# One decoder step on one core: three input projections in the loop that makes the token operands instead of two, with the raw tokens packed three pieces to a tile

## The chip, the core and the metric

The kernel runs on one core of one Trainium2 chip. A core has five engines with an instruction queue each: PE (TensorE, matmuls and weight loads), DVE (VectorE), ACT (ScalarE), POOL (GpSimd) and SP (SyncE, here only an issuer of DMAs); ACT and POOL issue DMAs too. The metric is the device time of one execution in microseconds (us); lower is better. Before, it is 1874.0 us, the median of three runs.

## What is computed

The reference is one inference step of a hybrid decoder layer for 1024 prompt tokens and 8 sample tokens, 1032 in all, of 1024 numbers each, in fp32. Cut to what this case touches:

```
def project_inputs(x, l, w):
    z = rmsnorm(x, w['attn_norm_g'][l]) @ w['w_in'][l]          # rmsnorm(x) = x * rsqrt(mean(x*x) + 1e-6) * gain
    q, kc, vc, ks, vs, kw, vw, nsa_g, pool_u, mem_q, merge_g = jnp.split(z, _split_points(), axis=-1)
    q = rmsnorm(q.reshape(b, t, KV_HEADS, GROUP, HEAD_DIM), w['nsa_q_g'][l])     # per head of 64
    ks = rmsnorm(kv(ks), w['nsa_ks_g'][l])
    kw = rmsnorm(kv(kw), w['nsa_kw_g'][l])
```

Behind it come three attention branches, a pooling mixer, a merge, an output projection and a feed-forward network; the change touches none of them.

## The kernel before

**Layout.** Tokens lie along the free axis, 1032 wide, in three chunks of 344 (`CH`); the 1024 features lie on 128 partitions in `KD` = 8 pieces (k = 0 to 7). Each fp32 operand is split into a high part and a low remainder in fp32r (a format of TensorE's), and each product is three matmuls: high weights by high tokens, high by low, low by high. One projection of 128 outputs over one chunk is thus 8 x 3 = 24 matmuls into one PSUM tile.

**The front.** The loop over chunks (L330 to L359) loads the raw tokens `xr` piece by piece (even k by SP, odd k by ACT), and makes of each piece: its high part `xh` on ACT (L338), its low part `xl` on DVE (L339), its square on POOL for odd k and on ACT for even k (L345, L347), and the running sum `ssq` of the squares on DVE for odd k and on POOL for even k (L348). The same loop runs two projections, ks and kw (weights `w_p[0]`, `w_p[1]`), over these operands: 2 x 24 matmuls for each chunk (L354). After a chunk, a matmul of `ssq` with ones (`ps_p`, L356) sums over the partitions, and `rsqrt` makes 1/rms of it in `rstd`: L273 on DVE, three ACT instructions (L274 to L276), L277 and L278 on DVE. Two multiplications by `rstd` bring the products into `z` (L359).

**Behind the front.** `hnorm` (from L368) normalises ks and kw per head; then four query projections q0 to q3 follow in `proj` (its matmuls are in `gemm`, L257; its low weights are L240, its multiplication by `rstd` L364), each with its `hnorm`. One unit of `hnorm` is one chunk of one projection: a square and a cast on ACT, a subtraction on POOL, two matmuls (L380), then `rsqrt` again and a final multiplication on DVE (L383). Six projections by three chunks make 18 units. Then come nine token blocks of the value projection (matmuls L257 with `wvh`, `wvl`), whose PSUM tiles DVE empties into `vtok` (L437) and `gate` (L438).

**Memory and order.** SBUF tiles of 1032 columns come from a ring of `NT` = 12 buffers, PSUM tiles from rings with tags g, s, t and p of 1, 3, 3 and 1 (`PSB`). Instructions are written in program order, and the framework's scheduler reorders them on each engine by a simulated timeline, so that an edit at one place moves rows elsewhere too.

Of the kernel before, what the change touches and what calls it, by code (L numbers as in the profile page):

```python
# [9 lines left out]
AF = mybir.ActivationFunctionType  # L10
ALU = mybir.AluOpType
# [5 lines left out]
KD = D // 128  # L17
# [4 lines left out]
CW = max(n for _, n in CH)  # L22
# [171 lines left out]
def body(nc, tc, xT, memT, w_p, w_m, w_v, w_mk, w_mv, w_up, w_un, w_out, w_gu, w_dn, w_pool, w_cmp, gains, consts, jlt,  # L194
         pg_k, pg_v, win_k, win_v, cm_k, cm_v, st_p, pt, ptv, o_y, o_k, o_v, o_wk, o_wv, o_pu, o_ps, o_mk, o_mv):
    from contextlib import ExitStack, nullcontext
    V, S, G, PE, SY = nc.vector, nc.scalar, nc.gpsimd, nc.tensor, nc.sync
    f = lambda a: a.bitcast(F32)
# [13 lines left out]
    def XG(name):  # L212
        return xgp.tile([128, T], F32R, name=name, tag="xg", bufs=16)
# [13 lines left out]
    ones = cp.tile([128, 128], F32, name="ones")  # L227
# [4 lines left out]
    def gv(n, i=0):  # L232
        return gn[:, _GW[n][0] + i:_GW[n][0] + i + 1]

    def psum(tag="s", dt=F32, w=512):
        return pp.tile([128, w], dt, name="ps_" + tag, tag=tag, bufs=dict(zip(('g', 's', 't', 'p'), PSB))[tag])

    def split(src, hi, lo, he=None, le=None):
        (he or S.copy)(hi, src)  # L239
        (le or V.tensor_sub)(lo, src, f(hi))  # L240

    def wload(src, n, eng=None, le=None, parts=1):
        wr = wp.tile([128, n], F32, name="wr", tag="wr", padded_shape=[128, T])
        (eng or SY).dma_start(wr, src)
        wh = wp.tile([128, n], F32R, name="wh", tag="wh", padded_shape=[128, 1024])
        wl = wp.tile([128, n], F32R, name="wl", tag="wl", padded_shape=[128, 1024])
        for i in range(parts):
            c = slice(n // parts * i, n // parts * (i + 1))
            split(wr[:, c], wh[:, c], wl[:, c], le=le)
        return wh, wl  # L250
# [31 lines left out]
    ca = A.enter_context(tc.tile_pool(name="cstA", bufs=1))  # L282
    CWID = consts.shape[1]
    ct = ca.tile([128, CWID], F32, name="ct")
    G.dma_start(ct, consts)

    def C(n):
        o, w, r = _CW[n]
# [7 lines left out]
    def TT(dt=F32, name="t"):  # L296
        return st_["tp"].tile([128, T], dt, name=name, tag="T", bufs=NT)
# [12 lines left out]
    def TX(name):  # L310
        return st_["tp"].tile([128, 512], F32R, name=name, tag="X", bufs=NX)
# [2 lines left out]
                                               engine=mybir.EngineType.Activation, ins=[], outs=[]))  # L314


    xh, xl, xr = [], [], []
    ssq = TT(name="ssq")
    rstd = cp.tile([128, T], F32, name="rstd")
    W01 = []  # L320
    ks, kw = TT(name="z"), TT(name="z")

    def xload(k, c):
        (SY, S)[k % 2].dma_start(xr[k][:, c], xT[k][:, c])

    for k in range(KD):
        xr.append(TT(name="xr"))
        xh.append(XG("xh"))
        xl.append(XG("xl"))
    for ci, (c0, n) in enumerate(CH):  # L330
        c = slice(c0, c0 + n)
        pss = [psum("st"[ci % 2])[:, :n] for _ in range(2)]
        for k in range(KD):
            xload(k, c)
            if ci == 0 and k < 2:
                W01.append(wload(w_p[k], 1024, parts=2))
            h, l = xh[k][:, c], xl[k][:, c]
            S.activation(h, xr[k][:, c], AF.Copy, scale=gv("attn", k))  # L338
            V.scalar_tensor_tensor(l, xr[k][:, c], gv("attn", k), f(h), op0=ALU.mult, op1=ALU.subtract)  # L339
            if k == 0:  # L340
                S.activation(ssq[:, c], xr[k][:, c], AF.Square)
            else:
                sq = TU("sq")[:, :n]
                if k in XG_SQ:
                    G.tensor_mul(sq, xr[k][:, c], xr[k][:, c])  # L345
                else:
                    S.activation(sq, xr[k][:, c], AF.Square)  # L347
                (G if k in XG_ADD else V).tensor_add(ssq[:, c], ssq[:, c], sq)  # L348
        for k in range(KD):
            for t in range(2):  # L350
                wh, wl = W01[t]
                w = slice(k * 128, k * 128 + 128)
                for x, (a, b) in enumerate(((wh, xh), (wh, xl), (wl, xh))):
                    PE.matmul(pss[t], lhsT=a[:, w], rhs=b[k][:, c], start=k == 0 and x == 0, stop=k == KD - 1 and x == 2)  # L354
        ps = psum("p")[:, :n]
        PE.matmul(ps, lhsT=ones, rhs=ssq[:, c], start=True, stop=True)  # L356
        rsqrt(tmp, rstd[:, c], ps, n, 1.0 / D)
        for t, z in enumerate((ks, kw)):
            V.tensor_mul(z[:, c], pss[t], rstd[:, c])  # L359

    def proj(i, src=None, tag="t"):
        wh, wl = wload((w_p if src is None else src)[i], 1024)
        z = TT(name="z")
        gemm(wh, wl, xh, xl, KD, lambda ci, c0, n, ps: V.tensor_mul(z[:, c0:c0 + n], ps, rstd[:, c0:c0 + n]),  # L364
             tag)
        return z
# [24 lines left out]
    ps = psum("g")  # L391
# [16 lines left out]
    qall = ca.tile([128, 64], F32, name="qall")  # L408
    V.memset(qall, 0.0)
    for j in range(4):  # L410
        q = proj(2 + j)
        hnorm(q, blk64, 1 / 64, gv("q"), split_sq=True)
        for s in range(2):
            h = 2 * j + s
            V.tensor_copy(qall[(h // 4) * 64:(h // 4) * 64 + 64, h * 8:h * 8 + 8], q[s * 64:s * 64 + 64, TP:T])
        SY.dma_start(qd[j], q)
# [5 lines left out]
    for a, b in ((0, 3), (3, 6), (6, 8)):  # L422
        n = (b - a) * 280
        r = TT(name="wvr")
        SY.dma_start(r[:, :n], w_v[:, a * 280:b * 280])
        h, l = TT(F32R, "wvh"), TT(F32R, "wvl")
# [4 lines left out]
    for t in range(9):  # L431
        m = 128 if t < 8 else NB
        c = slice(t * 128, t * 128 + m)
# [1067 lines left out]
```

## Time and profile before

| | before |
|---|---|
| median of three runs | 1874.0 us (1872.23 to 1876.44) |
| profiled execution | 1869.54 us |
| its span, first to last instruction | 1867.8 us |
| mean granted TensorE clock | 0.989 of full speed |
| PE busy | 1798.3 us, 96% of the span |
| DVE, ACT, POOL busy | 1210.0, 870.7, 737.5 us |
| first matmul | 7.67 us after the start |
| last matmul of the front (L354) | 48.27 us after the start |
| PE's next idle time behind it | before 116.08 us, 1.33 us long |

The profile is one execution seen by the hardware profiler; its time is 0.24% under the median of the three runs. PE is busy for nearly the whole span, so a change of the time has to come out of the idle time and the slow stretches that are left to PE. A row of the time line names its start in us, its length, the engine, the line of the code, and the operation as output<-inputs.

### The profile page before, as it was taken

Reading aid. Unit: us, or ns where it says so; the run is one execution under the profiler, and the core shown is the slowest. Engines: PE = TensorE matmul, PEld = TensorE weight load, DVE = VectorE, ACT = ScalarE, POOL = GpSimd, SP = SyncE. Lnnn points to the kernel's source line nnn. Section 1 sums busy time; section 2 is a strip of 40 time slices with the busy share of each in tenths; the row PEclk is TensorE's granted clock in tenths of the full one; section 3 lists DMA queues with packets and bytes.
Section 4 is the critical chain, followed back from the end, with each engine's and each line's share of the span. In section 5 each row is a group of like instructions: output and inputs, shape, how many; then the busy total and the mean of one; then the engine's idle time right before and its main releaser. Section 6 shows DMA issues by size and latency. Waiting matters only on the chain.

```text
span 1867.8 us, 34509 instructions
## 1 busy us (share of the span) xinstructions
PE 1798.3 (96%) x12337; PEld 1729.2 (93%) x12337; DVE 1210.0 (65%) x2748; ACT 870.7 (47%) x2012; POOL 737.5 (39%) x865
## 2 busy tenths in 40 slices
PE   6999999999999999989999999999999999999999
PEld 5998998888988999979989998899999999999999
DVE  8875788663564766778886834866666666636332
ACT  5643766445454676657774545422322223314100
POOL 5300211556341645457753437655545545100000
PEclk9999999899999999989999999999999999999999
DMA  4243124999665111552325643122222222546122
GB/s 162 100 148 139 65 101 164 296 316 315 205 201 169 53 43 63 179 165 78 108 64 177 213 134 100 62 87 78 71 80 80 84 87 69 170 131 184 59 69 94
DMA packets 142366, 241.13 MB, mean 129 GB/s; under 512 B 21449, under 2 KB 100450, under 8 KB 142194
## 3 DMA queue, kind: packets, MB, share of 16 engines
q1 hardware_dynamic: 118722, 189.69, 31.2%
q0 software_dynamic: 8496, 30.23, 4.8%
q10 hardware_dynamic: 14976, 19.01, 2.9%
q8 instruction: 97, 1.59, 0.4%
q14 instruction: 75, 0.61, 0.1%
HBM read 176.31 MB, written 62.55 MB: 128 GB/s over the span
## 4 chain that ended last, share of the span: by engine, by line
PE 55%; DMA 5%; DVE 4%; issue 2%; ACT 2%; POOL 1%; SPq 0%; ACTq 0%; DVEq 0%; POOLq 0%
PE ps_t L257 10%; PE ps_s L1385 10%; PE ps_t L1385 9%; PE ps_g L257 7%; PE ps_s L257 7%; PE ps_p L1061 3%; PE ps_s L1032 3%; PE ps_t L1077 2%; PE ps_g L1385 2%; PE ps_p L1385 2%; DMA mg<-acd 1%; DMA mg<-gd 1%; DMA gt<-gd 1%; DMA olr<-od 1%; DVE t L240 0%
## 5 line engine op out<-in xcount | busy, mean ns | idle before, releaser
L257 PE MATMUL ps_g<-xh,wh 128*128 128x344 f32 x624 | 206.1, 330 | 3.9 <-ACT mg L543 2.3
L257 PE MATMUL ps_g<-xl,wh 128*128 128x344 f32 x624 | 201.7, 323 | 0.0
L257 PE MATMUL ps_g<-xh,wl 128*128 128x344 f32 x624 | 201.6, 323 | 0.0
L239 ACT CAST wh<-wr 128x512 fp32r<-128x512 f32 (+3 forms) x138 | 99.9, 746 | 199.9 <-PE ps_t L257 83.5
L1051 POOL TENSOR_SCALAR P<-P,st,gate 128x384 f32<-128x384 f32 (+2 forms) x192 | 125.6, 664 | 94.6 <-DVE st L1046 37.8
L240 DVE TENSOR_TENSOR wl<-wr,wh 128x512 fp32r<-128x512 f32 (+3 forms) x112 | 105.0, 946 | 56.9 <-ACT wh L239 55.5
L239 ACT CAST cw<-tS 128x512 fp32r<-128x512 f32 x88 | 54.3, 619 | 182.0 <-PE ps_t L1385 98.2
L522 ACT ACTIVATE P<-P,st 128x384 f32<-128x384 f32 (+2 forms) x192 | 112.1, 586 | 40.1 <-DVE st L519 36.3
L257 PEld LDWEIGHTS ps_g<-xh,wh 128*128 128x128 f32 x624 | 118.2, 189 | 9.2 <-ACT mg L543 4.1
L257 PEld LDWEIGHTS ps_g<-xl,wh 128*128 128x128 f32 x624 | 118.5, 190 | 1.1 <-issue 0.4
L257 PEld LDWEIGHTS ps_g<-xh,wl 128*128 128x128 f32 x624 | 118.2, 189 | 1.3 <-issue 0.2
L240 DVE TENSOR_TENSOR ptl<-ps_t,pth 128x512 fp32r<-128x512 f32 (+1 forms) x208 | 108.0, 530 | 15.6 <-ACT pth L239 13.4
L239 ACT CAST pth<-ps_t 128x512 fp32r<-128x512 f32 (+1 forms) x208 | 91.3, 457 | 46.6 <-PE ps_t L1077 29.2
L240 DVE TENSOR_TENSOR cw<-tS,cw 128x512 fp32r<-128x512 f32 x88 | 93.3, 1061 | 29.7 <-ACT cw L239 26.1
L1385 PE MATMUL ps_s<-t,cw 128*128 128x258 f32 x792 | 106.1, 283 | 3.1 <-ACT rq L274 3.1
L1385 PE MATMUL ps_t<-t,cw 128*128 128x258 f32 x792 | 106.8, 283 | 2.1 <-DVE t L240 2.1
L1385 PE MATMUL ps_s<-b,cw 128*128 128x258 f32 x792 | 107.8, 286 | 0.0
L1385 PE MATMUL ps_t<-b,cw 128*128 128x258 f32 x792 | 105.6, 282 | 0.3 <-issue 0.3
L1385 PEld LDWEIGHTS ps_s<-t,cw 128*128 128x128 f32 x792 | 100.0, 190 | 3.3 <-ACT rq L274 3.3
L1385 PEld LDWEIGHTS ps_t<-t,cw 128*128 128x128 f32 x792 | 99.6, 189 | 2.9 <-DVE t L240 2.9
L1385 PEld LDWEIGHTS ps_s<-b,cw 128*128 128x128 f32 x792 | 101.4, 192 | 0.3
L519 DVE CUSTOM_DVE_ANT_0 P<-ps_s,ct 128x384 f32<-128x384 f32 (+3 forms) x160 | 83.2, 530 | 27.0 <-PE ps_t L1077 18.1
(527 smaller groups left out, 5659.0 us busy)
## 6 DMA issues: line engine op xcount, KB each, us to landing
kpg<-pg_k SPq DMA_DIRECT2D x128, 192.0 KB, 4.1
wr<-w_gu SPq DMA_DIRECT2D x44, 512.0 KB, 3.8
gd<-mg ACTq DMA_DIRECT2D x72, 172.0 KB, 3.4
wr<-w_m POOLq DMA_DIRECT2D x24, 512.0 KB, 5.4
acd<-zu SPq DMA_DIRECT2D x44, 258.0 KB, 2.0
mg<-acd SPq DMA_DIRECT2D x66, 172.0 KB, 3.0
mg<-gd SPq DMA_DIRECT2D x48, 172.0 KB, 2.4
wr<-w_p SPq DMA_DIRECT2D x16, 512.0 KB, 3.4
```

The lines of the kernel that those rows point to most:

```text
L239: (he or S.copy)(hi, src)
L240: (le or V.tensor_sub)(lo, src, f(hi))
L257: PE.matmul(ps, lhsT=x, rhs=y, start=i == 0, stop=i == n - 1)
L519: V.tensor_tensor_reduce(P[u], s, m, -scale, ini, ALU.add, ALU.min, st[:, u:u + 1])
L522: S.activation(P[u], P[u], AF.Exp, bias=nm, scale=-1.0, accum_out=st[:, 6 + u:7 + u])
L1032: PE.matmul(ps, lhsT=u["q"][:, i * 128:i * 128 + 128], rhs=kk[:, k0 * 128 + a:k0 * 128 + a + n], start=x == 0, stop=x == 1)
L1051: lastp[:] = [G.tensor_scalar(p_, p_, st4[:, j, 5:6], gate[:, q, c:c + 1], op0=ALU.mult, op1=ALU.mult)]
L1061: PE.matmul(pv[:, c0:c0 + n], lhsT=lh, rhs=rhs, start=pvs["n"] == 0, stop=last, skip_group_check=True)
L1077: PE.transpose(pt_[:, x * 128:x * 128 + 128], pd[y][:, o - offs[y]:o - offs[y] + 128], ident)
L1385: PE.matmul(ps[c], lhsT=a[:, x * 512 + k * 128:x * 512 + k * 128 + 128], rhs=b[k][:, y * HT + c * HC:y * HT + c * HC + HC], start=first an ...
```

## The change

Four edits, all in the front:

1. The raw tokens of one chunk are packed three pieces to one tile of 1032 columns, so three tiles a chunk in place of eight tiles for all chunks. The third chunk's second and third tile take the buffers of the first chunk's first two.
2. A third projection, q0 (weights `w_p[2]`), joins ks and kw in the loop. Its weights are loaded to a tile of their own (`wraw`) and split in two halves of 512 columns (`halves`). Its 24 matmuls of a chunk are written behind the 48 of the other two, and `ps_p` stands among them. The later `proj(2)` falls away.
3. The PSUM tiles of the chunks come from tags s, t, s; the three of a chunk take all three buffers of their tag.
4. The load of the constants `ct` is written behind the first chunk's operands, no longer ahead of the front. On POOL's queue it still stands second, right behind the load of the gains.

Matmuls, vector operations and bytes moved are the same in number, but for the split of q0's weights (two halves on each of ACT and DVE in place of one whole instruction).

```
-    G.dma_start(ct, consts)
...
     for ci, (c0, n) in enumerate(CH):
         c = slice(c0, c0 + n)
-        pss = [psum("st"[ci % 2])[:, :n] for _ in range(2)]
+        xt = [TT(name="xr") for _ in range(3)]
+        if ci == 0:
+            ssq = TT(name="ssq")
+            zs = [TT(name="z") for _ in range(3)]
+        pss = [psum("sts"[ci])[:, :n] for _ in range(2)]
         for k in range(KD):
-            xload(k, c)
+            xr = xt[k // 3][:, k % 3 * CW:k % 3 * CW + n]
+            (SY, S)[k % 2].dma_start(xr, xT[k][:, c])
...
+        if ci == 0:
+            SY.dma_start(raw[:, :1024], w_p[2])
+            W.append(halves(raw, lambda: TX("w2")))
+            G.dma_start(ct, consts)
+
+        def along(t, k):
+            wh, wl = W[t]
+            for x, (a, b) in enumerate(((wh, xh), (wh, xl), (wl, xh))):
+                PE.matmul(pss[t], lhsT=a(k), rhs=b[k][:, c], start=k == 0 and x == 0, stop=k == KD - 1 and x == 2)
+
         for k in range(KD):
             for t in range(2):
...
+                along(t, k)
+        pss.append(psum("sts"[ci])[:, :n])
+        for k in range(KD):
+            along(2, k)
+            if k == 3:
+                ps = psum("p")[:, :n]
+                PE.matmul(ps, lhsT=ones, rhs=ssq[:, c], start=True, stop=True)
         rsqrt(tmp, rstd[:, c], ps, n, 1.0 / D)
-        for t, z in enumerate((ks, kw)):
+        for t, z in enumerate(zs):
             V.tensor_mul(z[:, c], pss[t], rstd[:, c])
+    ks, kw, q0 = zs
...
-        q = proj(2 + j)
+        q = proj(2 + j) if j else q0
```

The lines move: the front's matmuls from L354 to L367, `xh` L338 to L348, `xl` L339 to L349, `ssq` L348 to L358, `ps_p` L356 to L377, its `z` L359 to L380, the token loads L324 to L343, `hnorm`'s L380 and L383 to L402 and L405, `vtok` and `gate` L437 and L438 to L459 and L460. What the scheduler makes of it is seen at three places.

**ACT, around the second chunk's token loads.** Before, ACT issues the loads of all three chunks (L324) between the casts of the first; `xr_161`, `xr_167`, `xr_173` and `xr_179` are the pieces k = 1, 3, 5 and 7, and the last rows shown are the last loads:

```order
L338 ACTIVATE xh_162<-xr_161,gn_139 128x344
L347 ACTIVATE sq_213<-xr_164 128x344
L324 DMA xr_161<-xT 128x344
L338 ACTIVATE xh_165<-xr_164,gn_139 128x344
L347 ACTIVATE sq_225<-xr_170 128x344
L324 DMA xr_167<-xT 128x344
L338 ACTIVATE xh_168<-xr_167,gn_139 128x344
L347 ACTIVATE sq_237<-xr_176 128x344
L324 DMA xr_173<-xT 128x344
L338 ACTIVATE xh_171<-xr_170,gn_139 128x344
L338 ACTIVATE xh_165<-xr_164,gn_139 128x344
L324 DMA xr_179<-xT 128x344
```

Of the changed kernel, these are the rows at the end of the first chunk; `ps_p_313` is that chunk's sum of squares, `xr_338` and `xr_339` are tiles of the second chunk:

```order
L348 ACTIVATE xh_167<-xr_173,gn_139 128x344
L239 CAST w2_243<-wraw_154 128x512
L348 ACTIVATE xh_169<-xr_173,gn_139 128x344
L239 CAST w2_247<-wraw_154 128x512
L274 ACTIVATE rq_a_328<-ps_p_313,epst_143 128x344
L275 ACTIVATE rstd_153<-rq_a_328 128x344
L276 ACTIVATE rq_a_328<-rstd_153 128x344
L343 DMA xr_338<-xT 128x344
L343 DMA xr_339<-xT 128x344
L348 ACTIVATE xh_155<-xr_338,gn_139 128x344
L351 ACTIVATE ssq_174<-xr_338 128x344
L343 DMA xr_339<-xT 128x344
```

The second chunk's loads on ACT now stand behind the three `rsqrt` instructions of the first.

**DVE, at the border of the first and the second chunk.** Before, around the first chunk's `rsqrt` (`rq_w_296`, and `rstd_155` with its two `z`), low parts and sums of the later chunks stand between its steps:

```order
L348 TENSOR_TENSOR ssq_154<-ssq_154,sq_339 128x344
L348 TENSOR_TENSOR ssq_154<-ssq_154,sq_435 128x344
L339 SCALAR_TENSOR_TENSOR xl_181<-xr_179,gn_139,xh_180 128x344
L712 TENSOR_SCALAR ptr_3815<-ptr_3815,ct_148 128x16
L277 TENSOR_TENSOR rq_w_296<-rq_w_296,rq_a_297 128x344
L348 TENSOR_TENSOR ssq_154<-ssq_154,sq_351 128x344
L278 SCALAR_TENSOR_TENSOR rstd_155<-rq_w_296,rstd_155 128x344
L348 TENSOR_TENSOR ssq_154<-ssq_154,sq_447 128x344
L359 TENSOR_TENSOR z_156<-ps_s_182,rstd_155 128x344
L359 TENSOR_TENSOR z_157<-ps_s_183,rstd_155 128x344
```

Of the changed kernel, `rq_w_327` is the first chunk's; `xr_338` is the second chunk's first tile:

```order
L358 TENSOR_TENSOR ssq_174<-ssq_174,sq_239 128x344
L273 TENSOR_SCALAR rq_w_327<-ps_p_313 128x344
L277 TENSOR_TENSOR rq_w_327<-rq_w_327,rq_a_328 128x344
L278 SCALAR_TENSOR_TENSOR rstd_153<-rq_w_327,rstd_153 128x344
L380 TENSOR_TENSOR z_175<-ps_s_178,rstd_153 128x344
L380 TENSOR_TENSOR z_176<-ps_s_179,rstd_153 128x344
L380 TENSOR_TENSOR z_177<-ps_s_300,rstd_153 128x344
L349 SCALAR_TENSOR_TENSOR xl_156<-xr_338,gn_139,xh_155 128x344
L358 TENSOR_TENSOR ssq_174<-ssq_174,sq_350 128x344
L349 SCALAR_TENSOR_TENSOR xl_158<-xr_338,gn_139,xh_157 128x344
```

All of `rsqrt` and three multiplications of the first chunk now stand ahead of the first low part of the second.

**PE, around the second chunk's `ps_p`.** Before, `ps_s_414` and `ps_s_415` are ks and kw of the third chunk; 24 matmuls of `ps_s_415` follow behind these rows, and then q0's projection:

```order
L354 MATMUL ps_s_414<-xh_180,wh_187 128x344
L354 MATMUL ps_s_414<-xl_181,wh_187 128x344
L354 MATMUL ps_s_414<-xh_180,wl_188 128x344
L356 MATMUL ps_p_402<-ssq_154,ones_141 128x344
L394 MATMUL ps_g_527<-ct_148,rstd_155 128x1 x2
L354 MATMUL ps_s_415<-xh_159,wh_199 128x344
L354 MATMUL ps_s_415<-xl_160,wh_199 128x344
L354 MATMUL ps_s_415<-xh_159,wl_200 128x344
```

Of the changed kernel, `ps_t_437` is the third projection of the second chunk, and `ps_s_478` the first of the third:

```order
L367 MATMUL ps_t_437<-xh_167,w2_248 128x344
L367 MATMUL ps_t_437<-xh_169,w2_247 128x344
L367 MATMUL ps_t_437<-xl_170,w2_247 128x344
L377 MATMUL ps_p_450<-ssq_174,ones_141 128x344
L367 MATMUL ps_t_437<-xh_169,w2_248 128x344
L367 MATMUL ps_s_478<-xh_155,wh_183 128x344
L367 MATMUL ps_s_478<-xl_156,wh_183 128x344
L367 MATMUL ps_s_478<-xh_155,wl_184 128x344
```

All 72 matmuls of the third chunk now stand behind the second chunk's `ps_p`, whose input is the sum `ssq` of that chunk. On DVE that sum's last addition (`ssq_174<-ssq_174,sq_386`) stands behind all but one of the third chunk's low parts, in these rows:

```order
L349 SCALAR_TENSOR_TENSOR xl_162<-xr_476,gn_139,xh_161 128x344
L349 SCALAR_TENSOR_TENSOR xl_164<-xr_476,gn_139,xh_163 128x344
L349 SCALAR_TENSOR_TENSOR xl_166<-xr_476,gn_139,xh_165 128x344
L349 SCALAR_TENSOR_TENSOR xl_168<-xr_477,gn_139,xh_167 128x344
L358 TENSOR_TENSOR ssq_174<-ssq_174,sq_386 128x344
L349 SCALAR_TENSOR_TENSOR xl_170<-xr_477,gn_139,xh_169 128x344
L358 TENSOR_TENSOR ssq_174<-ssq_174,sq_499 128x344
```

Behind the front, the first matmuls of `hnorm` (L402) stand 30 matmuls of the next projection behind the last of the front; before, the first one stands one matmul behind it (`ps_t_669` is then q0, now it is q1 in `ps_t_819` and `ps_t_845`).

## Rows read from the trace of the kernel before

**Rows 1.** The page's list of busy time by engine (us, share, instructions).

```profile
PE 1798.3 (96%) x12337; PEld 1729.2 (93%) x12337; DVE 1210.0 (65%) x2748; ACT 870.7 (47%) x2012; POOL 737.5 (39%) x865
```

**Rows 2.** PE's waits from 0 to 130 us: in total, times, longest.

```profile
PE ps_s L354 <- ACT xh L338: 7.7, 1, 7.7
PE ps_s L354 <- ACT wh L239: 3.0, 1, 3.0
PE ps_p L356 <- DVE ssq L348: 2.1, 1, 2.1
PE ps_t L354 <- DVE xl L339: 1.9, 3, 0.8
PE ps_t L257 <- DVE gate L438: 1.3, 1, 1.3
```

**Rows 3.** Windows: start:end and length, busy us (instructions) by engine, granted clock, DMA.

```profile
core 0: us, PE busy (x) PEld busy (x) DVE busy (x) ACT busy (x) POOL busy (x), PEclk, DMA share, GB/s
...
8.00:48.40 40.40, 31.61 (x152) 27.91 (x152) 36.53 (x55) 21.78 (x45) 24.46 (x22) 0.96 0.43 150
...
42.00:45.90 3.90, 3.90 (x14) 3.57 (x15) 3.90 (x7) 2.40 (x5) 2.50 (x2) 0.56 0.01 2
...
51.23:115.30 64.07, 63.52 (x413) 62.67 (x412) 54.84 (x103) 47.25 (x98) 17.58 (x17) 1.00 0.36 134
...
62.00:115.30 53.30, 52.75 (x341) 51.95 (x339) 47.75 (x87) 39.65 (x80) 15.09 (x14) 1.00 0.40 151
...
70.00:110.00 40.00, 40.00 (x267) 40.00 (x266) 38.41 (x70) 29.03 (x60) 11.28 (x10) 1.00 0.46 169
...
116.00:400.00 284.00, 270.29 (x1664) 253.76 (x1664) 201.32 (x510) 150.18 (x372) 66.31 (x124) 0.98 0.48 165
```

**Rows 4.** PE's time line at the front's end and the gate: start, length, idle before.

```profile
41.96 1.04 PE L356 MATMUL ps_p<-ssq,ones 128*128 128x344 f32 x2 [2.09 <-DVE ssq L348]
...
48.11 0.32 PE L354 MATMUL ps_s<-xl,wh 128*128 128x344 f32 x1
48.27 0.33 PE L354 MATMUL ps_s<-xh,wl 128*128 128x344 f32 x1
48.44 0.32 PE L257 MATMUL ps_t<-xh,wh 128*128 128x344 f32 x1
...
116.08 0.37 PE L257 MATMUL ps_t<-wvh,xh 128*128 128x280 f32 x1 [1.33 <-DVE gate L438]
```

**Rows 5.** Groups of instructions, 0 to 48 us: busy us, mean ns.

```profile
L339 DVE SCALAR_TENSOR_TENSOR xl<-xr,gn,xh 128x344 fp32r<-128x344 f32 x24 | 20.3, 880 | 0.7 <-ACT xh L338 0.4 <-DMA xr<-xT 0.3
L348 DVE TENSOR_TENSOR ssq<-ssq,sq 128x344 f32<-128x344 f32 x12 | 9.3, 777 | 0.8 <-POOL ssq L348 0.8
L240 DVE TENSOR_TENSOR wl<-wr,wh 128x512 fp32r<-128x512 f32 x4 | 3.2, 830 | 2.1 <-ACT wh L239 2.1
L274 ACT ACTIVATE rq_a<-ps_p,epst 128x344 f32<-128x344 f32 x2 | 1.1, 545 | 4.2 <-DVE rq_w L273 4.2
```

**Rows 6.** DVE's time line in the front, and its first `hnorm` and gate instructions.

```profile
8.65 0.57 DVE L339 SCALAR_TENSOR_TENSOR xl<-xr,gn,xh 128x344 fp32r<-128x344 f32 x1
...
13.09 1.07 DVE L339 SCALAR_TENSOR_TENSOR xl<-xr,gn,xh 128x344 fp32r<-128x344 f32 x1
...
17.78 4.22 DVE L339 SCALAR_TENSOR_TENSOR xl<-xr,gn,xh 128x344 fp32r<-128x344 f32 x4
...
43.44 0.50 DVE L273 TENSOR_SCALAR rq_w<-ps_p 128x344 f32<-128x344 f32 x1
...
51.23 0.51 DVE L273 TENSOR_SCALAR rq_w<-ps_s 128x344 f32<-128x344 f32 x1
...
115.30 0.48 DVE L437 TENSOR_SCALAR vtok<-ps_t,rtok 128x256 f32<-128x256 f32 x1
```

**Rows 7.** ACT's last token load of the front on its queue.

```profile
18.35 0.33 ACTq L324 DMA_DIRECT2D xr<-xT  x1
```

**Rows 8.** Token loads of the first 48 us by queue: count, KB, us to landing.

```profile
xr<-xT SPq DMA_DIRECT2D x12, 172.0 KB, 2.3
xr<-xT ACTq DMA_DIRECT2D x12, 172.0 KB, 3.8
```

**Rows 9.** DVE's groups from 48.4 to 116 us.

```profile
L364 DVE TENSOR_TENSOR z<-ps_t,rstd 128x344 f32<-128x344 f32 x12 | 6.1, 510 | 0.9 <-PE ps_t L257 0.8
L240 DVE TENSOR_TENSOR wl<-wr,wh 128x1024 fp32r<-128x1024 f32 x5 | 6.1, 1220 | 1.6 <-ACT wh L239 1.6
L359 DVE TENSOR_TENSOR z<-ps_s,rstd 128x344 f32<-128x344 f32 x2 | 0.9, 512 | 0.0
```

## What the change should do to the time

> **What bounds the kernel now.** The page's busy times come first [rows 1]: PE works for 96% of the span, so about 69 us of it are PE's own idle time, and the change can only win out of that, or out of stretches where PE runs slowly. PE's waits of the first 130 us [rows 2] show where it idles here. Before its first matmul it waits 7.7 us for the first `xh` and then 3.0 us for weights; after that the list is only DVE's: 3.5 us in all for low parts `xl`, and 2.1 us at the second chunk's `ps_p` for `ssq`. So the front's pace is set by DVE. The windows say the same [rows 3]: from 8 to 48.4 us DVE is busy for 36.5 of 40.4 us, PE for 31.6. And those 31.6 are not all at full speed: after the wait of 2.09 us at `ps_p` [rows 4] the granted clock is 0.56 of full speed between 42 and 45.9 us [rows 3], near the lower of its two levels, 1.2 of 2.4 GHz.
>
> From 48.44 us on, where the front's last matmul is out [rows 4], PE has work without a gap until it waits 1.33 us for DVE's `gate` at 116.08. Between, DVE is not idle either: 54.84 us of the 64.07 from the first `hnorm` step to the first evacuation of the value blocks, and 38.41 of 40 us (96%) from 70 to 110 [rows 3]. So two chains of nearly one length meet at 116 us: PE's matmuls, and DVE's `hnorm` steps. The change has to shorten both to win.
>
> **Step 1: what leaves PE behind the front.** q0's 72 matmuls move into the front. A matmul of this shape starts 0.16 us behind the one ahead (48.11, 48.27, 48.44) [rows 4]: 72 x 0.157 = 11.3 us. The third chunk's `ps_p`, which lies behind the front before and inside it now, is about 0.5 us more (half of the pair that takes 1.04 us in [rows 4]). So if the front now ends less than 11.8 us later than 48.4, that is before 60.2 us, PE gets to the gate earlier, else later. The change pays on PE only as far as the added matmuls fill idle time.
>
> **Step 2: when the front now ends.** I walk along DVE, which sets its pace. The first chunk: 8 low parts at 0.88 us, 4 sums at 0.78, and 6 halves of weights at 0.83 (two of them new, for q0) are 15.1 us [rows 5]; from about 8 us on [rows 6], with no wait for tokens, that is 23 us. Now comes the border of the chunks. In the order of before DVE goes on with later chunks there. In the new order it stands still: `ps_p` (0.5 us, in PE's queue behind nearly all of the third projection's 24 matmuls) and then `rsqrt` with three ACT instructions of 0.55 us or a little less [rows 5], 1.5 us together, leave it idle for about 3 us; its own L273, L277, L278 and three `z` of 0.5 us are 3 us more. That makes 29 us. On ACT the second chunk's odd loads stand behind the same `rsqrt`, so they go out at about 27 us where before the last of all three chunks was out at 18.35 [rows 7]; with 2.3 to 3.8 us to landing [rows 8] they are there at 29.5 to 31, which costs another 0.5 us. So the second chunk's first low part starts at 29.5 us.
>
> From there to the last sum of the second chunk DVE's order has 15 low parts and 5 sums: 13.2 + 3.9 = 17.1 us, so `ps_p` starts at 46.6 us; before it started at 41.96 [rows 4]. PE has nine matmuls for each piece now, 1.4 us, where DVE needs 1.1 to 1.3 for a piece's low part and its share of the sums: the second chunk's 72 go along from 30 us on and are out at 42 to 44 us, so PE waits, I estimate, 3 us for `ssq`, longer than the 2.09 us of before. Behind `ps_p` lie all 72 matmuls of the third chunk, the last of the second, and the third chunk's `ps_p`. At full clock that is 73 x 0.157 + 2 x 0.5 = 12.5 us and 0.6 us for the small products L416; and the slow stretch comes again: 14 matmuls in 3.9 us [rows 3] in place of 2.2, 1.7 us more. 46.6 + 12.5 + 0.6 + 1.7 = **61.4 us**, 1.2 us behind the 60.2 of step 1.
>
> The bounds: a low part takes 0.57 us where POOL rests and 1.07 where POOL works [rows 6]. 15 of them at 0.57 give 56.8 us for the front's end, at 1.07 64.3 us. The four in a row of 4.22 us [rows 6] stand near the upper price.
>
> **The rule that bears on that price.** The Trainium skill says on its page "SBUF — State Buffer", section "SBUF: two separate sides", that a VectorE instruction with two SBUF inputs and a GpSimd instruction that reads SBUF take one port pair in turn, whichever starts first holding it throughout. The two durations above agree with that. By the rule alone the front would end at the upper bound, since POOL's squares of the second chunk now start together with that chunk's low parts, and the time would be 1879.5 us.
>
> **Step 3: DVE's chain to the gate.** The first `hnorm` matmuls of the new order stand 30 matmuls behind the front's end, 4.7 us; before one matmul. So DVE's first `hnorm` step comes at about 61.4 + 5 = 66.4 us, where it came at 51.23 [rows 6]. From there it has less left than before: the 54.84 us of [rows 3] lose four multiplications of `proj` (2.0), the third chunk's two `z` (0.9), one whole weight remainder (1.2) [rows 9], and L277, L278 of the third chunk's `rsqrt` and the two `rtok` copies (1.4 by 0.5 us each): 5.5 us, 49.3 left. All 18 units of `hnorm` bar one still stand ahead of the first gate evacuation on DVE. At the 96% of the stretch 70 to 110 that takes 51.4 us: the evacuation starts at 66.4 + 51.4 = **117.8 us**, against 115.30 [rows 6], 2.5 us later. At the 90% of 62 to 115.3 (47.75 of 53.30) [rows 3] it takes 54.8 us, 5.9 us later. I take the higher share, as all units' squares are then long made and only DVE is short, and lean a little to the other: 3 us.
>
> PE arrives by step 2 at 114.75 + 1.2, about 116 us, so it waits there for DVE: the gate, not PE, decides, and the delay is 3 us. What follows is PE's: 270.3 of 284 us busy from 116 to 400 [rows 3], with waits on what is behind it in the same order, so the delay is carried to the end. Edits without a price: the packing moves the same 24 loads of 172 KB [rows 8]; the constants' load keeps its place on POOL's queue; the PSUM tags give each chunk three buffers, which the third chunk takes from the first, long multiplied by then.
>
> **The sum.** 1869.54 + 3 = 1872.5 us for an execution like the profiled one. That one lies 4.5 us under the median of the three runs, so against the median the forecast is 1874.0 + 3 = **1877 us**. 0.2% of it, 3.7 us, is about what a measurement of this kernel can tell from no change; the forecast is thus no change, leaning to slower.
>
> **Rivals.** *The front hides the third projection (faster).* The low parts of the later chunks come at their lower price, or the border costs less than I think: DVE's own work of the front, 8 + 36.5 us and 1.7 for the two halves, would let it end near 49 to 50 us. Then PE saves up to 11 us, and DVE's chain starts at 55, gate at 106: -10 us, 1864 us. It decides from a front that ends at 55.5 us: 60.5 + 51.4 = 111.9, 3.4 us won. Against it stand the order's rows at the border and at the second `ps_p`. Chance 0.22, with -4 to -6 us likelier than -10.
>
> *The gate comes later still (slower).* Low parts at the upper price put the front's end at 64.3 us and the gate at 69.3 + 51.4 = 120.7, 5.4 us later; DVE's share at 90% makes it 5.9, both 8.8. And PE, idle at the gate for 3 us and more, restarts at the lower clock, another 1.7 us by the same 14 matmuls. That is 1879.5 to 1884.5 us. It decides from a gate evacuation behind 119.0 us. For it: DVE's times beside POOL. Against it: each low part that finds POOL at rest gives 0.5 us back, and four of them 2 us. Chance 0.38.
>
> *The third projection does nothing.* It isn't "along" in the second and third chunk but a block behind the operands, PE neither gains nor loses, and DVE's chain has enough slack to keep 115.30: 0 us, 1874. It shares the forecast's side of the bound; together they have 0.40, of which the forecast 0.28.
>
> **How the numbers follow.** Faster 0.22, same 0.40, slower 0.38. Cutting off the far half of the faster case (beyond -7 us, 0.09) and the end of the slower one (beyond +11 us, 0.1) leaves 1867 to 1885 us. The likeliest case alone reaches from 1872 to 1880.
>
> **What would show it.** In the profile of the changed kernel: DVE idle for about 3 us in all at 22 to 29 us before L349 of the second chunk; ACT's second-chunk loads issued near 27 us; the second `ps_p` at 45 to 48 us behind a wait for `ssq` L358 of about 3 us and a granted clock near 0.5 after it; the last L367 at 60 to 63 us; DVE's first L459 at 116.5 to 120 us, PE waiting there for `gate` L460. The prediction is wrong if the last L367 lies before 56 us, if the gate's evacuation comes ahead of 114, or if behind 120 us the distance between the two kernels changes by more than 3 us.

## The result, and the profile after

The changed kernel takes 1884.48 us, the median of seven runs (1879.98 to 1891.65), beside 1874.6 us of seven runs of before: ratio 1.0053, 95% interval 1.0039 to 1.0067. It is **slower by 10 us**, half a per cent, and the interval leaves out 1. Run again on another chip (e8, below) it takes 1883.5 us beside 1870.91, ratio 1.0074 [1.0049, 1.0099]. The profiled execution is the slowest of the seven, 1891.65 us; that of e8 took 1880.15 us, so the two profiles stand near the two ends, and what both show is taken as the change's. Two executions of the experiments, 2391.68 us of e7 and 8641.79 us of e12, went at mean granted clocks of 0.681 and 0.185 and are left out of the ratios.

The page's busy times of the changed kernel, as [rows 1]:

```profile
PE 1805.6 (96%) x12337; PEld 1735.8 (92%) x12337; DVE 1218.4 (64%) x2749; ACT 873.1 (46%) x2013; POOL 735.7 (39%) x865
```

PE has as many instructions and 7 us more busy time in a span that is 22 us longer: part of the loss is idle time, part slower matmuls.

The front and the border of the chunks, DVE's time line of the changed kernel (start, length, idle before), as [rows 6]:

```profile
20.48 0.52 DVE L358 TENSOR_TENSOR ssq<-ssq,sq 128x344 f32<-128x344 f32 x1
25.65 0.52 DVE L273 TENSOR_SCALAR rq_w<-ps_p 128x344 f32<-128x344 f32 x1 [4.66 <-PE ps_p L377]
27.82 0.52 DVE L277 TENSOR_TENSOR rq_w<-rq_w,rq_a 128x344 f32<-128x344 f32 x1 [1.66 <-ACT rq_a L276]
...
30.21 0.62 DVE L349 SCALAR_TENSOR_TENSOR xl<-xr,gn,xh 128x344 fp32r<-128x344 f32 x1
...
66.42 0.94 DVE L273 TENSOR_SCALAR rq_w<-ps_s 128x344 f32<-128x344 f32 x2 [0.29 <-PE ps_s L402]
...
123.29 0.48 DVE L459 TENSOR_SCALAR vtok<-ps_t,rtok 128x256 f32<-128x256 f32 x1
```

DVE stands still for 6.3 us at the border (4.0 in e8's profile, 2.29 and 1.66 at the same two places). The second chunk's first low part starts at 30.21 us, the first `hnorm` step at 66.42 (before 51.23), the first evacuation of the value blocks at 123.29 (before 115.30).

PE's waits of the first 140 us, as [rows 2]:

```profile
PE ps_s L367 <- ACT wh L239: 8.1, 2, 6.9
PE ps_s L402 <- ACT rq_a L274: 5.2, 2, 3.3
PE ps_g L416 <- DVE rstd L278: 3.2, 1, 3.2
PE ps_p L377 <- DVE ssq L358: 3.0, 1, 3.0
PE ps_s L496 <- ACT rq_a L274: 1.2, 1, 1.2
```

and where they lie, PE's time line, as [rows 4]:

```profile
28.95 1.01 PE L416 MATMUL ps_g<-ct,rstd 128*128 128x1 f32 x4 [3.18 <-DVE rstd L278]
...
46.83 0.85 PE L377 MATMUL ps_p<-ssq,ones 128*128 128x344 f32 x2 [2.99 <-DVE ssq L358]
...
59.47 0.32 PE L367 MATMUL ps_s<-xh,w 128*128 128x344 f32 x1
...
113.24 0.58 PE L402 MATMUL ps_s<-mg,blkr 128*128 128x344 f32 x2 [3.28 <-ACT rq_a L274]
115.70 0.94 PE L402 MATMUL ps_s<-mg,blkr 128*128 128x344 f32 x2 [1.87 <-ACT rq_a L274]
117.87 6.77 PE L496 MATMUL ps_s<-sq,ones 128*128 128x256 f32 x16 [1.23 <-ACT rq_a L274]
```

The front ends 11.2 us later than before with 11.8 us of work more in it, so PE comes to 110 us as early as before. There it waits 6.4 us in three pieces. It doesn't wait at `gate` any more (0.6 us in e8's profile), but a little ahead of it, at matmuls of `hnorm` and of the memory branch (L496): their PSUM tiles of tag s are still held by earlier `hnorm` units, until ACT's L274 has read them. The windows, as [rows 3], show what comes on top:

```profile
66.42:123.30 56.88, 50.49 (x305) 48.28 (x304) 50.47 (x92) 41.94 (x85) 15.67 (x16) 0.92 0.36 132
70.00:110.00 40.00, 39.97 (x266) 39.55 (x264) 36.48 (x64) 30.11 (x62) 12.39 (x14) 1.00 0.45 162
112.00:126.00 14.00, 9.65 (x32) 7.62 (x33) 13.00 (x30) 8.47 (x16) 0.00 (x0) 0.63 0.24 95
```

From 112 to 126 us the granted clock is 0.63, between its two levels of 2.4 and 1.2 GHz: part of the stretch ran at the lower one. Both traces have 12337 matmuls, so they can be laid side by side by their count: the changed kernel is 1.0 us ahead of before at 107 us and 8.3 us behind at 125; in e8's profile 3.2 us ahead and 5.8 behind. So the gate costs some 9 us: the 6.4 us of waits and some 4 for the slow stretch, less the 1.33 us that before waits there too.

**Behind the gate.** By the same count the distance is 7.4 us at 700 us in the one profile and 2.5 us in the other. Then, in the selected and windowed attention, both lose some 8 us: they are 15.2 and 10.7 us behind at 896 us. PE idles from 800 to 900 us for 12.1 us (11.4 in e8's profile), 5.1 before, summed over its time line. Behind 896 us the slower of the two loses another 6.9 us, and e8's nothing. The waits of e8's profile from 800 to 900 us:

```profile
PE ps_p L1083 <- DVE st L1065: 2.8, 1, 2.8
PE ps_g L257 <- DVE mg L1231: 2.3, 2, 1.5
PE ps_p L1083 <- DVE ptl L240: 2.0, 1, 2.0
```

DVE's and POOL's time lines of the changed kernel there:

```profile
852.66 2.50 DVE L547 SCALAR_TENSOR_TENSOR st<-st,ct 128x1 f32<-128x1 f32 x1
...
856.04 3.23 DVE L547 SCALAR_TENSOR_TENSOR st<-st,ct 128x1 f32<-128x1 f32 x1
...
852.45 2.66 POOL L1226 TENSOR_TENSOR mg<-mg,rstd 128x344 f32<-128x344 f32 x3
855.12 1.20 POOL L1073 TENSOR_SCALAR P<-P,st,gate 128x256 f32<-128x256 f32 x2
856.28 0.91 POOL L1226 TENSOR_TENSOR mg<-mg,rstd 128x344 f32<-128x344 f32 x1
857.19 1.19 POOL L1073 TENSOR_SCALAR P<-P,st,gate 128x512 f32<-128x512 f32 x2
858.35 0.90 POOL L1226 TENSOR_TENSOR mg<-mg,rstd 128x344 f32<-128x344 f32 x1
```

An instruction of one column takes 2.5 and 3.23 us. The first ends with three POOL instructions (L1226), behind which POOL goes on at once with L1073; the second ends with the last POOL row shown. In the kernel before none of them is over 1.2 us.

### The profile page after: what moved, and what is told of

It reads as the page before. It is cut to its first block, busy times and chain, and to the rows that moved or that the text cites. A ratio compares the mean times of both kernels' runs of the same rounds, so it can differ in the third digit from the quotient of the medians.

```text
span 1889.9 us, 34507 instructions
## 1 busy us (share of the span) xinstructions
PE 1805.6 (96%) x12337; PEld 1735.8 (92%) x12337; DVE 1218.4 (64%) x2749; ACT 873.1 (46%) x2013; POOL 735.7 (39%) x865
## 4 chain that ended last, share of the span: by engine, by line
PE 70%; DMA 11%; DVE 9%; issue 4%; ACT 3%; POOL 1%; SPq 0%; POOLq 0%; ACTq 0%; DVEq 0%
PE ps_t L257 15%; PE ps_g L257 11%; PE ps_s L1407 10%; PE ps_t L1407 9%; PE ps_s L257 6%; PE ps_p L1083 3%; DMA kpg<-pg_k 3%; PE ps_s L1054 3%; PE ps_t L1099 3%; PE ps_p L257 2%; PE ps_g L1407 2%; PE ps_p L1407 2%; DMA mg<-acd 1%; PE ps_s L367 1%; DMA vpg<-pg_v,ptr 1%
## 5 line engine op out<-in xcount | busy, mean ns | idle before, releaser
L257 PE MATMUL ps_g<-xh,wh 128*128 128x344 f32 x600 | 197.5, 329 | 7.2 <-ACT mg L565 4.2
L257 PE MATMUL ps_g<-xh,wl 128*128 128x344 f32 x600 | 193.6, 323 | 0.4 <-DVE wl L240 0.4
L257 PE MATMUL ps_g<-xl,wh 128*128 128x344 f32 x600 | 193.8, 323 | 0.0
L1073 POOL TENSOR_SCALAR P<-P,st,gate 128x384 f32<-128x384 f32 (+2 forms) x192 | 125.4, 662 | 102.0 <-DVE st L1068 55.4
L257 PEld LDWEIGHTS ps_g<-xh,wh 128*128 128x128 f32 x600 | 113.3, 189 | 13.3 <-ACT mg L565 6.1
L257 PEld LDWEIGHTS ps_g<-xh,wl 128*128 128x128 f32 x600 | 113.1, 189 | 2.6 <-DVE wl L240 0.7
L257 PEld LDWEIGHTS ps_g<-xl,wh 128*128 128x128 f32 x600 | 113.4, 189 | 1.9 <-issue 0.5
L1407 PE MATMUL ps_t<-t,cw 128*128 128x258 f32 x792 | 106.8, 283 | 2.2 <-DVE t L240 2.2
L1407 PEld LDWEIGHTS ps_t<-b,cw 128*128 128x128 f32 x792 | 99.1, 188 | 0.7 <-issue 0.6
```

The costliest lines, as they stand in the source:

```text
L257: PE.matmul(ps, lhsT=x, rhs=y, start=i == 0, stop=i == n - 1)
L1073: lastp[:] = [G.tensor_scalar(p_, p_, st4[:, j, 5:6], gate[:, q, c:c + 1], op0=ALU.mult, op1=ALU.mult)]
L1407: PE.matmul(ps[c], lhsT=a[:, x * 512 + k * 128:x * 512 + k * 128 + 128], rhs=b[k][:, y * HT + c * HC:y * HT + c * HC + HC], start=first an ...
```

## The experiments

All were timed in five rounds beside the kernel before on the same chip. "Behind at 200 us" is how far PE lies behind the kernel before's profiled execution at the same count of matmuls, past the gate and past all `hnorm` matmuls that e1, e5, e6, e10 and e12 move; a minus is ahead.

| run | us, before on that chip | ratio [95%] | last front matmul, first `hnorm`, first `vtok` (us) | behind at 200 us |
|---|---|---|---|---|
| changed | 1884.48, 1874.6 | 1.0053 [1.0039, 1.0067] | 59.5, 66.4, 123.3 | 8.5 |
| e8 changed again | 1883.5, 1870.91 | 1.0074 [1.0049, 1.0099] | 57.3, 64.2, 121.1 | 5.7 |
| e1 `hnorm` of q3 later | 1881.25, 1872.71 | 1.005 [1.0034, 1.0067] | 56.0, 63.0, 112.6 | 3.7 |
| e2 border | 1872.08, 1872.71 | 0.9997 [0.9982, 1.0011] | 48.3, 55.6, 113.8 | -1.0 |
| e3 packing only | 1876.07, 1872.71 | 1.0012 [0.9995, 1.0029] | 46.9, 52.2, 115.1 | -0.6 |
| e4 third projection only | 1887.37, 1872.71 | 1.0076 [1.0059, 1.0092] | 60.3, 67.3, 124.2 | 9.9 |
| e5 border, `hnorm` of q2, q3 later | 1865.75, 1870.91 | 0.9967 [0.995, 0.9984] | 48.6, 55.8, 98.5 | -11.3 |
| e6 before, `hnorm` of q2, q3 later | 1868.79, 1870.91 | 0.9983 [0.9967, 0.9998] | 47.5, 50.4, 108.1 | -2.6 |
| e7 ring of six | 1899.09, 1870.91 | 1.014 [1.0117, 1.0164] | 57.3, 64.2, 115.9 | 2.1 |
| e9 one tensor input | 1880.57, 1872.38 | 1.0049 [1.0032, 1.0066] | 55.9, 62.8, 119.7 | 5.0 |
| e10 e5 and e9 | 1860.72, 1872.38 | 0.9936 [0.9917, 0.9956] | 48.3, 55.6, 98.2 | -11.0 |
| e11 before, one tensor input | 1870.12, 1872.38 | 0.9975 [0.9958, 0.9992] | 48.6, 51.5, 116.1 | 2.7 |
| e12 `hnorm` of q2, q3 later | 1869.05, 1872.7 | 0.9982 [0.997, 0.9994] | 58.8, 65.7, 106.8 | -3.6 |

The front of one order ends at 55.9 to 59.5 us from profile to profile (changed, e1, e8, e9, e12); differences of 3 us in the last column between such runs are this spread. The profiled execution of before, 1869.54 us, is itself on the fast side of its kernel.

**e1, e12: `hnorm` moved behind the value blocks.**

```
     for j in range(4):
         q = proj(2 + j) if j else q0
-        hnorm(q, blk64, 1 / 64, gv("q"), split_sq=True)
...
+        qs.append(q)
+        if j < 3:        # e12: j < 2
+            qfin(j)      # hnorm, copies, store of q
...
         SY.dma_start(vd[t * 128:t * 128 + m, :], v[:m])
+        if t == 8:
+            for j in range(3, 4):   # e12: range(2, 4)
+                qfin(j)
```

> The changed kernel with the hnorm of the last query projection written behind the value blocks; nothing else is edited. Theory A (the loss sits at the gate: DVE's chain of 18 hnorm units comes out late, and PE stands behind hnorm matmuls that wait for it, 6.4 us in three waits between 113 and 118 us, and then runs at half clock): three units no longer stand ahead of the gate, the waits shrink to under 2 us and the half clock goes, 8 to 10 us less than the changed kernel, 1874 to 1877 us. Theory B (the loss comes later, from the order behind 400 us and the page loads): no change, 1882 to 1886 us.

> The changed kernel with only the hnorm of the last two query projections behind the value blocks, the border left as it is. If the two losses are separate (the border keeps PE from winning 11 us in the front, the gate costs 7 to 10 more): the gate's loss goes whole, PE passes it 1 to 4 us ahead of before, and the time is 8 to 10 us over the 1865.8 of both edits, 1872 to 1877 us. If the gate alone made the loss and the border is free: 1865 to 1868 us.

With three units moved PE still waits 4.8 us at L402 for a PSUM tile of tag s, now with fewer units behind it, and the time is by the medians, each beside before's on its chip, 1 to 4 us better, which the intervals don't tell apart: less than theory A expected. That too few units are moved is what e12 then tests. With six moved there is no wait from 60 to 140 us; PE's waits of e12 up to 140 us:

```profile
PE ps_s L367 <- ACT wh L239: 6.9, 1, 6.9
PE ps_g L416 <- DVE rstd L278: 3.2, 1, 3.2
PE ps_p L377 <- DVE ssq L358: 2.7, 1, 2.7
PE ps_s L367 <- DVE xl L349: 0.4, 1, 0.4
```

All of the change's loss goes, and 3.6 us more: 1869.05 us with the border's idle time still there. That the gate holds a loss, and that it goes with these units, is shown. Beside before's on their chips e12 lies 13 to 16 us below the changed kernel, which is more than the gate's 9: e12's profile has only 5.4 us of PE idle from 800 to 900 us, although one L547 (here L558) is long in it too:

```profile
838.17 2.26 DVE L558 SCALAR_TENSOR_TENSOR st<-st,ct 128x1 f32<-128x1 f32 x1
```

So its gain is that of the gate and of the other loss together.

**e2: `rsqrt` of the first chunk behind the second chunk's operands.**

```
+        if ci == 1:
+            with tc.issue_after(ih.ins), tc.issue_after(il.ins):   # last xh, xl of the chunk
+                fin()              # rsqrt and the three z of chunk 0
...
-        rsqrt(tmp, rstd[:, c], ps, n, 1.0 / D)
-        for t, z in enumerate(zs):
-            V.tensor_mul(z[:, c], pss[t], rstd[:, c])
+        if ci:
+            fin()
```

> The changed kernel with the first chunk's rsqrt and its three z written behind the second chunk's operands, so that DVE and ACT go on with low and high parts at the border. Theory A with the border as its source: DVE's 8 us of idle and late work at 20.5 to 30 us go down to 2, the front's last matmul comes at 53 to 55 us instead of 59.5, the first hnorm step at 60 instead of 66.4, the first gate evacuation at 117 to 119 instead of 123.3; 4 to 7 us less than the changed kernel, 1877 to 1880 us. If the hnorm chain's pace alone sets the gate (its start does not matter): the front ends earlier but the gate does not, 1883 to 1885 us. Theory B: 1882 to 1886 us.

The front does what the change is for: its 216 matmuls end at 48.34 us, where 144 ended at 48.27 before. PE is then 11.7 us ahead (at 90 us), and gives 10.7 of them back. The kernel's own time line of PE:

```profile
48.34 0.32 PE L370 MATMUL ps_s<-xh,w 128*128 128x344 f32 x1
...
103.78 0.58 PE L409 MATMUL ps_s<-mg,blkr 128*128 128x344 f32 x2 [2.56 <-ACT rq_a L274]
106.24 0.94 PE L409 MATMUL ps_s<-mg,blkr 128*128 128x344 f32 x2 [1.87 <-ACT rq_a L274]
108.42 6.73 PE L503 MATMUL ps_s<-sq,ones 128*128 128x256 f32 x16 [1.24 <-ACT rq_a L274]
```

The front ends 11 us earlier than the changed kernel's, more than I expected (5 us), and the first `vtok` comes 9.5 us earlier; the time is that of before, where I expected 1877 to 1880 us.

**e3, e4: one part of the change alone.** e3 leaves out the third projection (`zs` of two, `proj(2)` as before); e4 leaves out the packing (`xt = [TT(name="xr") for _ in range(KD)]` once, q0's raw weights in two tiles of 512 columns).

> Only the packing: raw tokens three pieces to a tile, the load of the constants written later, two projections in the front, q0 projected later as before. The order shows the same standstill at the border as in the changed kernel. If the packing's border makes the loss: the front's last matmul at 52 to 55 us instead of 48.3, the gate 3 to 6 us later than before, 1878 to 1882 us. If the third projection makes it: 1873 to 1876 us, the kernel before.

> Only the third projection: raw tokens in eight tiles as before, q0's weights loaded in two halves to the smaller tiles, three projections in the front. The order shows low parts of all chunks interleaved as before, with no standstill at the border. If the border of the packed tiles makes the loss: the front's last matmul at 52 to 56 us, the gate at or ahead of 117, 1868 to 1876 us. If the third projection makes it (hnorm starts later whatever the border): the gate at 120 or later, 1880 to 1885 us.

The packing alone costs nothing that the measurement can tell: it has the border too (DVE idles 3.4 us there, PE waits 3.6 us for `rstd`), but with two projections PE has slack for it, and the front ends where it did. e4 costs as much as the change, though its order has no border. Of both pairs of expectations the branch that laid the loss on the border was wrong, and the other came near. But e4 doesn't price the third projection by itself. In it q0's weights are loaded behind all tokens, their low half is made on DVE at 37 us, and the third projection stands behind that. Its PE waits up to 140 us:

```profile
PE ps_s L369 <- ACT xh L348: 6.7, 1, 6.7
PE ps_s L369 <- DVE w L240: 5.0, 1, 5.0
PE ps_s L404 <- ACT rq_a L274: 4.4, 2, 2.4
```

And of its loss only half lies at the gate: it is 9.9 us behind at 200 us and 16.9 at 700, for a reason that was not looked for.

**e5, e6: both edits; and the second on the kernel before.** e5 has e2's and e12's edits; e6 has e12's on the kernel before.

> Both edits at once: the first chunk's rsqrt behind the second chunk's operands, and the hnorm of the last two query projections behind the value blocks. Theory A (the packed front can give PE its 11 us, and the hnorm chain takes them back at the gate): with six units fewer ahead of it the gate is no longer late, PE keeps the 11.7 us that it led with the first edit alone, 9 to 12 us less than before, 1861 to 1864 us. Theory C (whatever is won ahead of the gate is lost behind it, as the six units only come later): 1870 to 1874 us.

> The kernel before with the same move of the last two query projections' hnorm behind the value blocks, as a control. Theory A: only the 1.33 us at the gate can be won, 1870 to 1873 us against 1872.7. If the move by itself is worth more, as a cure for something that both kernels have: under 1868 us.

With the gate freed PE keeps 11.3 of its 11.7 us at 200 us, and 15.0 at 700; 5.2 us are left at the end, less than the 9 to 12 expected, since e5 loses 9 us between 700 and 896 us, where the two long L547 stand again (9.0 us of PE idle from 800 to 900 us). The control wins 2.1 us and leads by 2.6 at 200 us, the spread of such runs. So about 9 of e5's 11.3 us at 200 us need the edits in the front.

**e7: more buffers for `rsqrt`.** `NT, NH, NU, NX = 12, 4, 10, 6` becomes `12, 6, 8, 6`.

> The changed kernel with six in place of four buffers in the ring that rsqrt's work tiles share (each hnorm unit takes three), and eight in place of ten in the ring of the squares, as the memory has no room for more. Theory D (that ring, not DVE's work, sets the pace of 57 us from the first hnorm step to the gate): the chain takes 50 to 53 us, the gate's evacuation at 117 to 119 us, 4 to 7 us less than the changed kernel, 1877 to 1880 us. If DVE's work sets it: 56 to 58 us, 1882 to 1887 us.

Theory D holds for the chain: 51.7 us from the first `hnorm` step to the first evacuation, 56.9 in e8 on the same chip, with DVE at work for 48.54 of them. The order is not the same: with six buffers the scheduler puts steps of the next unit between those of one, and two DVE instructions fewer stand ahead of the evacuation. The window of e7, and that of e8:

```profile
64.22:115.90 51.68, 48.26 (x308) 46.79 (x306) 48.54 (x90) 40.39 (x85) 17.69 (x16) 1.00 0.40 146
```

```profile
64.22:121.10 56.88, 50.50 (x308) 48.20 (x306) 50.48 (x92) 41.94 (x85) 15.66 (x16) 0.94 0.37 132
```

As a kernel it is 15.6 us slower than e8: from 800 to 1070 us PE is busy for 247.1 us in place of 253.4, and from 778 to 1000 us it falls behind before by some 25 us more. That the two missing buffers of the other ring do it is likely, as the attention takes its tiles there, but was not tried; three L547 of 2.7 to 3.4 us stand there as well. So e7 doesn't separate the two rings, nor the ring from the new order.

**e8: the changed kernel once more.**

> The changed kernel unedited, once more, beside the others on their chip, to see how much of the first profile's 22 us was that execution's own. Theory A: 10 us behind before at the gate again, and at the end a median 9 to 12 us above before's; the profiled execution's further 12 us from 800 to 1100 us are not there again. If they are the change's: a profile 20 us above before's.

It is 5.8 us behind past the gate, less than the 10 expected, as it came there 3.2 us ahead, and its idle time from 800 to 900 us is there again; the profile as a whole lies 10.6 us behind before's, so some 11 of the first profile's 22 us were that execution's own.

**e9, e10, e11: the small instruction.**

```
-            V.scalar_tensor_tensor(st[:, 6:7], st[:, 3:4], extra[1], st[:, 6:7], op0=ALU.mult, op1=ALU.add)
+            V.tensor_scalar(st[:, 6:7], st[:, 3:4], extra[1], st[:, 6:7], op0=ALU.mult, op1=ALU.add)
```

> The changed kernel with one small DVE instruction written otherwise, far behind the front: in the selected and windowed attention, st = st * w + st over one column (L547) as a scalar_tensor_tensor with two tensor inputs becomes a tensor_scalar with one tensor input and two per-partition scalars; the numbers are the same. In both profiles of the changed kernel two of its 30 executions took 2.5 and 3.2 us at 848 to 859 us, beside a train of POOL instructions, where the others take about 0.3, and PE waited there 7 us for what stands behind them. Theory E (a DVE instruction with two inputs in SBUF is held up for as long as POOL's train runs, and that is the loss behind the gate): none of them over 0.5 us, PE's idle time from 800 to 900 us down from 11 or 12 us to 5 to 7, and 4 to 6 us less than the changed kernel, 1877 to 1880 us. If they only wait for another reason: no change, 1882 to 1886 us.

> All three edits on the changed kernel: the first chunk's rsqrt behind the second chunk's operands, the hnorm of two query projections behind the value blocks, the small instruction with one tensor input. With theories A and E both right the gains add up: 5 us below before from the first two as measured, 4 to 6 more, 1860 to 1863 us beside a before of 1872. If E is wrong: 1865 to 1868 us.

> The kernel before with only the small instruction rewritten. Its profile has none of these instructions over 1.2 us, so theory E expects nothing: within 2 us of before. If the rewriting by itself is worth something: 3 us or more below.

The 32 executions from 400 to 1100 us, of the changed kernel and of e9:

```profile
L547 DVE SCALAR_TENSOR_TENSOR st<-st,ct 128x1 f32<-128x1 f32 x32 | 15.5, 489 | 2.5 <-ACT st L546 2.5
```

```profile
L547 DVE TENSOR_SCALAR st<-st,ct 128x1 f32<-128x1 f32 x32 | 8.3, 266 | 2.7 <-ACT st L546 2.4
```

and of before, where the line is L525:

```profile
L525 DVE SCALAR_TENSOR_TENSOR st<-st,ct 128x1 f32<-128x1 f32 x32 | 10.6, 336 | 2.2 <-ACT st L524 1.7
```

In e9 the 7 us are gone on DVE, PE's wait for L1065 is not in the list, and its idle time from 800 to 900 us is 8.3 in place of 11.4 us, still 3 us over before's and more than theory E expected (5 to 7): the long instructions are some 3 of the 6 to 7 us. The time is 8.2 us over before's on its chip, where the changed kernel's is 9.9 and 12.6 over: 2 to 4 us less, within the intervals. On top of e5 the edit is worth 5 to 7 us by the medians (the two intervals overlap a little), and e10 with 1860.72 us beats both kernels: 0.9936 of before. On before itself it wins 2.3 us, where I expected nothing beyond 2: the mean is 336 ns there, so shorter waits of the same kind are probably in it too.

## Why the prediction was right and wrong

The range held the time, by 0.5 us, and the sign of the lean was right; the forecast of "no change, leaning to slower" was not, nor the band of the likeliest case, 1872 to 1880 us. By its steps:

- **What bounds it**: two chains that meet at 116 us. Right, and it decided: e2 gives PE 11.7 us and the time doesn't move until e5 and e10 free the other chain.
- **Step 1**, 11.3 us of matmuls: right; e2's PE lead is 11.7 us.
- **Step 2**, the front's end at 61.4 us: measured 59.47 (57.27 in e8), below my 60 to 63. `ps_p` started at 46.83 (46.6), behind a wait of 2.99 (3), and the loads went out at 27.31 (27), but partly by luck: DVE was done with the first chunk at 21.0 us, not 23, and the border took that back, 6.3 us of idle time in place of 3. The 15 low parts ahead of the second chunk's last sum took 0.96 us on average, between the two prices and nearer the upper. The term that was too large is what follows `ps_p`: 12.64 us in place of 14.8. The small products L416 stand behind the front and not in it, and the slow stretch did not come in this execution. In e8's it did, with 14.15 us from `ps_p` to the front's end. The windows of the two:

```profile
46.83:59.47 12.64, 12.64 (x77) 12.24 (x78) 7.50 (x13) 5.21 (x9) 2.78 (x3) 1.00 0.11 32
```

```profile
43.10:57.30 14.20, 14.19 (x77) 13.79 (x78) 7.52 (x13) 5.23 (x9) 2.76 (x3) 0.88 0.10 31
```

- **Step 3 failed.** The first `hnorm` step came at 66.42 (66.4), by luck: the front ended 1.9 us early, and the step came 7.0 us behind it and not 5. The work left was 50.5 us (49.3), but DVE did it in 56.88 us, at a share of 89% and not 96%: 5.5 us more than the 51.4 summed. I took the share of before's stretch from 70 to 110 us, which leaves out both ends of the chain. In before's DVE was busy for 12.6 of the 18.8 us from 51.23 to 70, and the changed kernel has such ends too: of its 6.4 us of idle time 3.3 lie ahead of 80 us and 1.8 behind 107, where the last six units stand alone in the order. 2.9 us of it are waits for a unit's own ACT steps (L276). e7 points to why DVE doesn't take the next unit meanwhile: with six buffers the scheduler puts the next unit's steps between, and the chain takes 51.7 us at a share of 94%. That this is near my 51.4 is in part chance, as two instructions fewer are in it.
- **The price at the gate** was in the wrong case. I let PE wait 3 us and go on, and put the slow clock into the rival. It waited 6.4 us, and the stretch of 0.63 clock cost some 4 more; before's own wait of 1.33 us goes off.
- **"Carried to the end, in the same order"** failed too. Behind 183 us PE's matmuls stand in another order than before, up to 974 us, and PE idles 6 to 7 us more from 800 to 900; two small DVE instructions held up beside trains of POOL are some 3 us of that (e9), and the rest is not explained. The prediction named "a change of more than 3 us behind 120 us" as a way to be wrong, and had no term for it.
- **The rivals.** The slower one is what happened, by its mechanism at the gate (low share, slow clock) and not by low parts at the upper price; its 1879.5 to 1884.5 us holds the median. That is partly luck: of the distance at the end of the two profiles (22.1 and 10.6 us) some 8 us come from the attention, which no rival names. The faster one's first half exists (e2) and its second does not: the gate does not follow the front.

The change itself does not force that second loss. In e1, e2, e4 and e12, which all have the third projection in the front, PE's matmuls stand from 655 us on in just before's order, and PE idles from 800 to 900 us for 5.4 to 7.2 us. One L547 of 2.26 to 2.36 us is in e2, e3, e4, e6 and e12, also without the change (e6), and those runs lose no more than some 3 us between 700 and 896 us. In e5 and e7 to e10 the order differs from before's until 970 us or later, as in the changed kernel.

What stays open: what e1 loses besides (its profiled execution, of 1874.82 us, is the fastest of its six, so it doesn't show what the median of 1881.25 pays), what the changed kernel's slower executions lose behind 900 us, which of the two rings does what in e7, and which edits bring the other order in the attention.

## What to carry to other kernels

Filling one engine's idle time pays only as far as the chain that it meets next can follow: look for the next point at which it waits for another engine, and ask whether that chain starts earlier too; here the front's 11 us could be had, and were worth nothing until 6 of 18 `hnorm` units had been taken from ahead of the gate. A chain's busy share is to be read from the part of it that will be left alone, not from where other work fills its waits. And under a scheduler that reorders the whole program, a local edit can have a second, unrelated price of several microseconds elsewhere, so that parts are to be judged at their own place in the trace as well as by the total.

## What the runs showed of the hardware

A DVE instruction of one column (128x1) with two tensor inputs in SBUF took 2.50 and 3.23 us beside POOL, against a mean of 0.27 us for the same arithmetic with one tensor input (e9). In the second case it started at 856.04 us, while a POOL instruction ran (L1073, until 856.32), and ended at 859.27, with the last of the four POOL instructions that followed that one (859.25). The Trainium skill says on its page "SBUF — State Buffer", section "SBUF: two separate sides", that such a DVE instruction and a POOL instruction that reads SBUF take turns at a port pair, and that whichever starts first holds it for the whole instruction. The trace agrees that DVE is held up; it was held for several POOL instructions in a row, and not for one alone.
